# A hybrid decoder step on one core: two plain pairs of gates per layer, branch inputs and adaLN computed under the gate pairs, sigmoids reloaded by GpSimd's queue

## The chip, the cores and the metric

The kernel runs on one core of a Trainium2 chip. The metric is the device time of one execution in microseconds. The core has a matrix engine (TensorE, PE in the profile; PEld is its loading of weights), three engines for element-wise work (VectorE or DVE, ScalarE or ACT, GpSimd or POOL) and SyncE (SP), which only issues transfers here. Each engine runs its own instructions in its own order and waits on semaphores for the others.

## The reference

One inference step of two layers over 1088 tokens (1024 of a prompt, 8 sequences of 8 new tokens), width 1024, all in float32:

```
def _trunk_layer(x, c, ...):
    shift, scale, gate = jnp.split(jax.nn.silu(c) @ w_ada + b_ada, 3, axis=-1)     # adaLN
    h = _rmsnorm(x, norm_g) * (1.0 + scale[:, None]) + shift[:, None]
    (qa, ka, va, ga, ub, vb, gb, qc, fc, ic, gc, ma, mb, mc) = _split_cols(h @ w_in, IN_SIZES)
    ya, ... = _window_attention(...)     # branch A, width 512
    yb = _spatial_gating(ub, vb, w_spatial, b_spatial)     # branch B, width 512
    yc, s_new = _hgrn2(...)     # branch C, width 512
    merged = (jax.nn.sigmoid(ma) * ((ya * jax.nn.silu(ga)) @ w_br_a)
              + jax.nn.sigmoid(mb) * ((yb * jax.nn.silu(gb)) @ w_br_b)
              + jax.nn.sigmoid(mc) * ((yc * jax.nn.silu(gc)) @ w_br_c))
    x = x + gate[:, None] * (merged @ w_out)
```

The parts that the change touches are the merge gates ma, mb, mc (3 x 1024 columns of h @ w_in, then a sigmoid), the gated branch inputs y * silu(g) of the first two branches, adaLN, and the merge.

## The kernel before

**Layout and arithmetic.** Activations lie with channels on the 128 partitions and tokens along the row. The 1088 tokens are cut into three column chunks of 384, 384 and 320 (`CH`). Every float32 product is made of three matmuls in a reduced format (`mm3`, L377 to L379): operands are split into a rounded part and a rest, by a cast on ScalarE and a subtraction on VectorE (`split`, L454 and L455; for weights `piece`, L341 and L342; for branch inputs L1422 and L1423).

**Stages of a layer.** After the branches come three stages. In the *gate stage* 24 tiles of 128 columns are computed in 12 pairs; each result goes through a sigmoid and is stored to DRAM (`put_gate`, L1299 and L1300). Pair e = 0 is plain: 96 matmuls of 384 columns and 48 of 320. Pairs e = 2 to 22 (`gate_pair`) treat the first two column chunks and the two halves of the depth as 2 x 2 blocks and use a Strassen-Winograd scheme with seven block products instead of eight: 84 matmuls of 384 columns and 48 of 320. It needs sums of operand blocks (`sums`, made once per layer on VectorE and POOL and split, tiles `sb`) and, for every pair, sums of its weight blocks (`gate_prefetch`, four operations on POOL, L1340 to L1343, split by `split_t` into tiles `tw`). Tiles `su` hold the partial results; the names u2, u3 and p5 in the code are parts of them.

In the *merge stage* each of the three branches has 8 tiles of 3 column chunks with 12 matmuls each. Its input comes from `load_y`: y and its gate branch g are loaded from DRAM (tiles `yr` and `gr`), multiplied (L1417), and split into tiles `y` or into a spare `H`. The inputs of the first branch are loaded when the gate stage is over, those of the next one under the matmuls of the present one. For each group of 12 matmuls `load_gate` (L1465) reloads a stored sigmoid two groups ahead, VectorE multiplies it with the result (L1496 in the first branch, L1498 later), POOL adds it to `mg` (L1499), and in the last branch the sum is split for the w_out product. In layer 0 the adaLN products of L289 (its own last third and all of layer 1's) run between the merge's matmuls, with weights loaded at L299, and are transposed at L276 after a copy at L272. The *w_out stage* follows.

**What sets the order.** POOL and SP run in the order in which the program is written; a scheduler orders PE, VectorE and ScalarE. All loads and nearly all stores of these stages are issued by SP, so a transfer that waits for data holds back those behind it. Work on the side is a list of generators, `side`; `pump()` advances the first two of them by one step, and `drain()` runs them to their end. Large tiles share 17 slabs (`slab`); raw weights have 4 buffers (`wr`), sigmoids 4 (`gq`), and PSUM has four banks for products and four for other uses.

## Time and profile before

| | us |
|---|---|
| three runs | 2409.55, 2403.61, 2394.68 |
| median | 2403.61 |
| the profiled execution | 2400.19 |
| its span | 2398.4 |
| PE busy | 2277.0 (95%) |
| VectorE, ScalarE, POOL busy | 1293.5, 806.3, 573.7 (54%, 34%, 24%) |
| Strassen pairs of layer 0 and 1 | about 674 to 923, 1877 to 2127 |
| merge of layer 0 and 1 | about 935 to 1145, 2138 to 2298 |

The profile is that of one execution; 1.8 us of its time lie outside the span. Times in its rows are counted from the start of the span. The mean clock granted to PE is 0.983 of full speed. PE's busy time counts a matmul from its start to a modelled end, and matmuls overlap, so the distance between starts tells what one costs, not its duration. A row of stages gives for one stretch of time the busy time of each engine with the number of instructions, then the granted clock, the share of the 16 DMA engines that was busy, and the rate of transfer.

### The profile page before, as it was taken

What the parts mean: (1) busy time and instruction counts of PE and PEld (TensorE: products, weight loads), DVE (VectorE), ACT (ScalarE), POOL (GpSimd) and SP (SyncE); (2) the same over time, 40 slices, a digit from 0 to 9 for tenths busy, and PEclk for the clock granted to TensorE, in tenths of its full rate; (3) what the DMA queues carried; (4) which work ended last, traced back from release to release, by engine and by line L of the source; (5) the groups of instructions that cost most, each with busy time, mean ns of one, the idle gap of its engine ahead of it and who ended that gap; (6) DMA issues with size and microseconds to landing.
All of it is one profiled execution on the core that took longest, in us unless ns stands there. A gap on an engine that the chain in (4) does not pass through costs nothing.

```text
span 2398.4 us, 43921 instructions
## 1 busy us (share of the span) xinstructions
PE 2277.0 (95%) x17402; PEld 2154.5 (90%) x17402; DVE 1293.5 (54%) x2897; ACT 806.3 (34%) x2044; POOL 573.7 (24%) x571
## 2 busy tenths in 40 slices
PE   6999999999989997998999999999999899979999
PEld 5999899989989997777999998999899899979999
DVE  6558656655364444445573586576553644346441
ACT  4445523333134332212233456223331333332220
POOL 3101013242232331133111010132422333212421
PEclk9999999999989998999999999999999899999999
DMA  7222111122123226766432221112221222355451
GB/s 278 75 81 75 62 40 55 57 70 80 58 71 109 93 93 232 238 191 187 163 98 71 82 73 53 51 47 65 63 77 47 89 95 93 106 222 176 132 199 46
DMA packets 140734, 251.31 MB, mean 105 GB/s; under 512 B 19760, under 2 KB 78384, under 8 KB 140496
## 3 DMA queue, kind: packets, MB, share of 16 engines
q1 hardware_dynamic: 129296, 209.96, 27.0%
q0 software_dynamic: 11232, 38.55, 4.5%
q8 instruction: 137, 2.24, 0.4%
q14 instruction: 69, 0.57, 0.1%
HBM read 185.13 MB, written 65.27 MB: 104 GB/s over the span
## 4 chain that ended last, share of the span: by engine, by line
PE 72%; DVE 11%; issue 6%; DMA 5%; POOL 3%; ACT 2%; SPq 1%; POOLq 0%; DVEq 0%; ACTq 0%
PE mm L377 14%; PE mm L378 14%; PE mm L379 14%; PE mm L431 4%; PE mm L433 4%; PE mm L432 4%; PE c L377 3%; PE c L379 3%; PE c L378 3%; DMA wr<-in_w_ada 1%; PE av L912 1%; PE sc L875 1%; POOL mg L1499 1%; DVE pc L342 1%; DMA gr<-y 1%
## 5 line engine op out<-in xcount | busy, mean ns | idle before, releaser
L377 PE MATMUL mm<-H,pc 128*128 128x384 f32 (+1 forms) x1792 | 599.5, 335 | 0.0
L378 PE MATMUL mm<-H,pc 128*128 128x384 f32 (+1 forms) x1792 | 589.4, 329 | 0.0
L379 PE MATMUL mm<-H,pc 128*128 128x384 f32 (+1 forms) x1792 | 588.2, 328 | 0.0
L342 DVE TENSOR_TENSOR pc<-wr,pc 128x512 fp32r<-128x512 f32 x308 | 220.9, 732 | 392.4 <-ACT pc L341 390.9
L377 PEld LDWEIGHTS mm<-H,pc 128*128 128x128 f32 x1792 | 336.7, 188 | 18.1 <-issue 15.1
L378 PEld LDWEIGHTS mm<-H,pc 128*128 128x128 f32 x1792 | 337.0, 188 | 5.6 <-issue 5.0
L379 PEld LDWEIGHTS mm<-H,pc 128*128 128x128 f32 x1792 | 336.6, 188 | 0.9 <-issue 0.4
L341 ACT CAST pc<-wr 128x512 fp32r<-128x512 f32 x312 | 190.2, 620 | 238.0 <-DMA wr<-in_w_br 80.6
L431 PE MATMUL mm<-pc,H 128*128 128x256 f32 x896 | 260.3, 291 | 0.2 <-DVE gq L1148 0.2
L433 PE MATMUL mm<-pc,H 128*128 128x256 f32 x896 | 255.7, 285 | 0.0
L432 PE MATMUL mm<-pc,H 128*128 128x256 f32 x896 | 255.0, 285 | 0.0
L433 PEld LDWEIGHTS mm<-pc,H 128*128 128x128 f32 x896 | 173.1, 193 | 3.2 <-issue 3.2
L431 PEld LDWEIGHTS mm<-pc,H 128*128 128x128 f32 x896 | 173.1, 193 | 2.2 <-DVE gq L1148 0.5
L432 PEld LDWEIGHTS mm<-pc,H 128*128 128x128 f32 x896 | 173.1, 193 | 0.0
L377 PE MATMUL mm<-y,pc 128*128 128x384 f32 (+1 forms) x384 | 132.0, 345 | 39.0 <-ACT y L1422 24.6
L1499 POOL TENSOR_TENSOR mg<-mg,gq 128x384 f32<-128x384 f32 (+1 forms) x96 | 98.9, 1037 | 228.6 <-DVE gq L1498 217.0
L455 DVE TENSOR_TENSOR tw<-wr,tw 128x512 fp32r<-128x512 f32 x88 | 82.7, 975 | 97.0 <-ACT tw L454 97.0
L378 PE MATMUL mm<-y,pc 128*128 128x384 f32 (+1 forms) x384 | 131.3, 342 | 0.3 <-DVE pc L342 0.3
L379 PE MATMUL mm<-y,pc 128*128 128x384 f32 (+1 forms) x384 | 129.2, 336 | 0.0
L377 PEld LDWEIGHTS mm<-y,pc 128*128 128x128 f32 x384 | 74.9, 195 | 46.1 <-ACT y L1422 26.5
L377 PE MATMUL c<-H,pc 128*128 128x320 f32 x352 | 109.6, 311 | 0.0
L379 PE MATMUL c<-H,pc 128*128 128x320 f32 x352 | 109.4, 311 | 0.0
(412 smaller groups left out, 4483.5 us busy)
## 6 DMA issues: line engine op xcount, KB each, us to landing
wr<-in_w_in SPq DMA_DIRECT2D x192, 256.0 KB, 3.6
g<-gq SPq DMA_DIRECT2D x96, 192.0 KB, 1.9
gq<-g SPq DMA_DIRECT2D x96, 192.0 KB, 3.1
wr<-in_w_ada SPq DMA_DIRECT2D x64, 256.0 KB, 3.9
wr<-in_w_in SPq DMA_DIRECT2D x112, 128.0 KB, 2.8
yr<-y SPq DMA_DIRECT2D x24, 544.0 KB, 7.0
wr<-in_w_br SPq DMA_DIRECT2D x48, 256.0 KB, 3.5
gr<-y SPq DMA_DIRECT2D x16, 544.0 KB, 7.9
```

Of the source, the lines that this page charges most:

```text
L341: S.copy(pc[:, 0, :], flat)
L342: eng.tensor_sub(pc[:, 1, :], flat, pc[:, 0, :].bitcast(F32))
L377: T.matmul(ps, w[0], r[0], start=start, stop=False, skip_group_check=True)
L378: T.matmul(ps, w[1], r[0], start=False, stop=False, skip_group_check=True)
L379: T.matmul(ps, w[0], r[1], start=False, stop=stop, skip_group_check=True)
L431: T.matmul(p3(ps), a, wh[k], start=k == 0, stop=False)
L432: T.matmul(p3(ps), a, wl[k], start=False, stop=False)
L433: T.matmul(p3(ps), b, wh[k], start=False, stop=k == 7)
L455: V.tensor_sub(dst_l, src, dst_h.bitcast(F32))
L875: T.matmul(ps[:, j * 256:j * 256 + w], lq, KS[a][hl][:, k0:k0 + w], start=hl == 0, stop=hl == 1)
L912: T.matmul(po[64 * a:64 * a + 64, :], v[:, vt:vt + 64], PT[a][:, c:c + 512], start=hb == 0, stop=hb == nh - 1, tile_position=(0, 64 * a))
L1499: G.tensor_add(mg, mg, sg)
```

## The change

1. Two pairs per layer are plain, e = 0 and e = 2; Strassen pairs are e = 4 to 22. `sums` is advanced once per group of matmuls over both.
2. `gating` computes 0.5 * y * g for the first two branches in 24 chunks per layer and stores the results to new DRAM tiles `yg`; `ada_wide` does adaLN with two column tiles in one matmul (256 columns, half as many instructions), its weights loaded in slabs (`wada`). Both are put on `side` when the Strassen pairs begin, and `pump()` now stands in every product of a pair, nine times per pair. In the merge no adaLN is left, and `load_y` only loads and splits.
3. `first_y` loads and splits the inputs of the first branch inside the last pair, behind the product that is last to use the operand sums.
4. `load_gate` issues the reloads of sigmoids from GpSimd's queue instead of SP's.
5. The last adds of the third branch (j = 7) go to VectorE.

```diff
--- before.py
+++ after.py
@@ -1288,6 +1288,7 @@
 
 
 
+        yg = [dp.tile([4, 128, NTOK], F32, tag=f"yg{l}{b}", name=f"yg{l}{b}") for b in range(2)] + [yd[2]]
         gd = [dp.tile([8, 128, NTOK], F32, tag=f"g{l}{b}", name=f"g{l}{b}") for b in range(3)]
         sbl = []
         HB = H[1]
@@ -1356,13 +1357,15 @@
 
         def gate_pair(e, w, last):
             blk = sbl[0]
+            sb = lambda x: [(blk[k, x, 0], blk[k, x, 1]) for k in range(4)]
+            s2, s3, s4 = [lambda k, x=sb(x): x[k] for x in range(3)]
             a = lambda c, k: (H[c][:, 0, k, :], H[c][:, 1, k, :])
-            sb = lambda x: lambda k: (blk[k, x, 0], blk[k, x, 1])
             full = lambda ps: ps[:, 0:384]
 
             def product(ps, ws, rs, start=True, stop=True):
                 for k in range(4):
                     mm3(ps, ws(k), rs(k), start and k == 0, stop and k == 3)
+                pump()
 
             tmp = slab("su")
             u2, u3, p5 = [tmp[:, x * 384:x * 384 + 384] for x in range(3)]
@@ -1373,14 +1376,17 @@
                 gate_prefetch()
             S.copy(u2, p1)
             x = full(mbank())
-            product(x, t2, sb(0))
+            product(x, t2, s2)
             V.tensor_add(u2, u2, x)
             c21 = full(mbank())
-            product(c21, t3, sb(1))
+            product(c21, t3, s3)
             V.tensor_add(u3, u2, c21)
             x12 = full(bank("c12"))
-            product(x12, lambda k: col(w, 8, 1, k + 4), sb(2))
-            pump()
+            product(x12, lambda k: col(w, 8, 1, k + 4), s4)
+            if last:
+                del blk, s2, s3, s4
+                sbl[:] = []
+                next(ly)
             x = full(mbank())
             product(x, t1, lambda k: a(1, k))
             S.copy(p5, x)
@@ -1406,52 +1412,107 @@
                     product(p1, lambda k: col(w, 8, 0, k + 4), lambda k: a(0, k + 4), start=False)
                     put_gate(e, 0, p1)
 
-        def load_y(b, dst, eng):
-
+        def gating():
+
+            for b in range(2):
+                for kk in range(4):
+                    for c, (t0, n) in enumerate(CH):
+                        t = slab("gy")
+                        y, g = t[:, 0:n], t[:, 384:384 + n]
+                        nc.sync.dma_start(y, yd[b][kk][:, t0:t0 + n])
+                        nc.sync.dma_start(g, yd[3 + b][kk][:, t0:t0 + n])
+                        yield
+                        V.scalar_tensor_tensor(y, y, 0.5, g, ALU.mult, ALU.mult)
+                        nc.sync.dma_start(yg[b][kk][:, t0:t0 + n], y)
+                        del t, y, g
+                        yield
+
+        def ada_wide(l, kts):
+
+            for p in range(0, len(kts), 2):
+                t = [slab("wada")[:, 0:1024].rearrange("p (a c n) -> p a c n", a=2, c=4) for _ in range(2)]
+                for e in range(2):
+                    for a in range(2):
+                        nc.sync.dma_start(t[e][:, a], i["w_ada"][l, kts[p + a]][:, 4 * e:4 * e + 4])
+                yield
+                yield
+                ps = bank("ada")
+                for e in range(2):
+                    for c in range(4):
+                        T.matmul(v3(ps[32 * c:32 * c + 32, 0:256], 128), cT[:, 4 * e + c, :], t[e][:, :, c],
+                                 start=e == 0, stop=e == 1, tile_position=(0, 32 * c))
+                del t
+                yield from ada_rows(l, kts[p:p + 2], ps)
+
+        def load_y(b, dst, first=False):
+
+            def half(y, kk, c):
+                t0, n = CH[c]
+                hi, lo = dst(kk, c)
+                x = y[:, t0:t0 + n]
+                S.copy(hi, x)
+                V.tensor_sub(lo, x, hi.bitcast(F32))
+
+            def load(kk):
+                y = slab("yr")
+                nc.sync.dma_start(y[:, 0:NTOK], yg[b][kk])
+                return y
+            if first:
+                ys = [load(kk) for kk in range(4)]
+                for c in range(3):
+                    for kk in range(4):
+                        half(ys[kk], kk, c)
+                return
             for kk in range(4):
-                y = slab("yr")
-                nc.sync.dma_start(y[:, 0:NTOK], yd[b][kk])
-                if b < 2:
-                    g = slab("gr")
-                    nc.sync.dma_start(g[:, 0:NTOK], yd[3 + b][kk])
-                    eng.tensor_mul(y[:, 0:NTOK], y[:, 0:NTOK], g[:, 0:NTOK])
-                h_ = 0.5 if b < 2 else 1.0
-                for c, (t0, n) in enumerate(CH):
-                    hi, lo = dst(kk, c)
-                    x = y[:, t0:t0 + n]
-                    S.mul(hi, x, h_)
-                    V.scalar_tensor_tensor(lo, x, h_, hi.bitcast(F32), ALU.mult, ALU.subtract)
+                y = load(kk)
+                yield
+                for c in range(3):
+                    half(y, kk, c)
                 yield
 
         def y_slabs():
             t = [[slab("y", F32R) for _ in range(2)] for _ in range(4)]
             return lambda k, c: [x[:, CH[c][0]:CH[c][0] + CH[c][1]] for x in t[k]]
 
+        def first_y():
+            y0.append(y_slabs())
+            for _ in load_y(0, y0[0], True):
+                pass
+            yield
+
+        y0 = []
+        ly = first_y()
+        sg_ = sums()
+        side.append(sg_)
         for e in range(0, 24, 2):
             w = unit()
-            if e == 0:
-                sg_ = sums()
-                side.append(sg_)
-                for j in range(2):
-                    for c in (2, 0, 1):
-                        def ev_s(c, t0, n, ps):
-                            put_gate(j, c, ps)
-                        f_group(w, j, 8, rhs_h, c, ev_s, 2)
-                        if j == 0 and c == 2:
-                            gate_prefetch()
+            if e > 2:
+                gate_pair(e, w, e == 22)
+                continue
+            first_group = True
+            for j in range(2):
+                for c in (2, 0, 1):
+                    def ev_s(c, t0, n, ps):
+                        put_gate(e + j, c, ps)
+                    f_group(w, j, 8, rhs_h, c, ev_s)
+                    if first_group:
+                        (gate_prefetch if e else prefetch)()
+                        first_group = False
+            if e == 2:
                 drain(sg_)
                 for k in range(4):
                     split(HB[:, 0, k, :], HB[:, 1, k, :], sbl[1][k])
                 sbl[1] = None
                 split_t()
-            else:
-                gate_pair(e, w, e == 22)
-        sbl[:] = []
+                side.append(gating())
+                if l == 0:
+                    side.append(ada_wide(0, list(range(16, 24))))
+                if l + 1 < L:
+                    side.append(ada_wide(l + 1, list(range(24))))
         tw[:] = []
+        drain(*side)
         prefetch()
-        rhs_y = y_slabs()
-        ly = load_y(0, rhs_y, V)
-        drain(ly)
+        rhs_y = y0[0]
 
 
         merged, sgs = [], []
@@ -1462,23 +1523,19 @@
                 b, j, c = grp.pop(0)
                 t0, n = CH[c]
                 sgs.append(small("gq", 384, bufs=4)[:, 0:n])
-                nc.sync.dma_start(sgs[-1], gd[b][j][:, t0:t0 + n])
+                nc.gpsimd.dma_start(sgs[-1], gd[b][j][:, t0:t0 + n])
         for _ in range(2):
             load_gate()
         for b in range(3):
             if b == 0:
                 Hy = new_H()
                 rhs_n = lambda k, c, Hy=Hy: (Hy[c][:, 0, k, :], Hy[c][:, 1, k, :])
-                ly = load_y(1, rhs_n, G)
+                ly = load_y(1, rhs_n)
                 side.append(ly)
-                if l == 0:
-                    side.append(ada(0, list(range(16, 24)), True))
             elif b == 1:
                 rhs_n = y_slabs()
-                ly = load_y(2, rhs_n, V)
-                side.insert(0, ly)
-                if l + 1 < L:
-                    side.append(ada(l + 1, list(range(24)), True))
+                ly = load_y(2, rhs_n)
+                side.append(ly)
             else:
                 del Hy
                 Hm = new_H()
@@ -1496,14 +1553,14 @@
                         V.tensor_mul(mg, sg, ps)
                         return
                     V.tensor_mul(sg, sg, ps)
-                    G.tensor_add(mg, mg, sg)
+                    (V if b == 2 and j == 7 else G).tensor_add(mg, mg, sg)
                     if b == 2:
                         split(Hm[c][:, 0, j, :], Hm[c][:, 1, j, :], mg)
                 f_mtile(w, j % 2, 4, lambda c, k: rhs_y(k, c), ev_m)
             if b < 2:
                 drain(ly)
                 rhs_y = rhs_n
-        del rhs_y, rhs_n, merged, ly
+        del rhs_y, rhs_n, merged, ly, y0
         drain(*side)
         last = l + 1 == L
         if not last:
```

The order that results shows at three places. First SP's queue in layer 0, around the loads of weights for pair e = 8 (`wr`); `g` rows are stores of sigmoids. Before:

```order
L1300 DMA g_7362<-gq_8018 128x384
L1300 DMA g_7362<-gq_8046 128x320
L338 DMA wr_8063<-in_w_in 128x512
L338 DMA wr_8068<-in_w_in 128x512
L338 DMA wr_8073<-in_w_in 128x512
L338 DMA wr_8078<-in_w_in 128x512
```

And now, where `gy` are the chunks of y and g, `yg` the product's store and `wada` the adaLN weights:

```order
L1301 DMA g_7364<-gq_8078 128x384
L1301 DMA g_7364<-gq_8106 128x320
L1422 DMA gy_8109<-y_271 128x384
L1423 DMA gy_8109<-y_274 128x384
L1426 DMA yg_7362<-gy_8109 128x384
L1436 DMA wada_8145<-in_w_ada 128x512 x2
L1436 DMA wada_8146<-in_w_ada 128x512 x2
L338 DMA wr_8151<-in_w_in 128x512
L338 DMA wr_8156<-in_w_in 128x512
L338 DMA wr_8161<-in_w_in 128x512
L338 DMA wr_8166<-in_w_in 128x512
```

Two loads, a store that waits for VectorE and four adaLN loads now stand between the stores of a pair and the next weights.

Second, SP's queue at the end of layer 0's gate stage, last Strassen pair to first branch. Before:

```order
L1300 DMA g_7364<-gq_9800 128x384
L1300 DMA g_7364<-gq_9828 128x320
L338 DMA wr_9831<-in_w_br 128x512
L338 DMA wr_9836<-in_w_br 128x512
L1413 DMA yr_9849<-y_271 128x1088
L1416 DMA gr_9851<-y_274 128x1088
```

And now:

```order
L1301 DMA g_7366<-gq_10146 128x320
L1458 DMA yr_10213<-yg_7362 128x1088
L1458 DMA yr_10215<-yg_7362 128x1088
L1458 DMA yr_10217<-yg_7362 128x1088
L1458 DMA yr_10219<-yg_7362 128x1088
L1301 DMA g_7366<-gq_10260 128x384
L1301 DMA g_7366<-gq_10265 128x384
L1301 DMA g_7366<-gq_10281 128x384
L1301 DMA g_7366<-gq_10309 128x320
L1301 DMA g_7366<-gq_10324 128x384
L1301 DMA g_7366<-gq_10352 128x320
L338 DMA wr_10355<-in_w_br 128x512
```

The four loads of the branch input moved ahead of the last pair's six stores; the first branch weight is still behind the last of them.

Third, ScalarE in one Strassen pair of layer 0 (`su` rows are copies of the first and the fifth product; `pc` and `tw` are casts of the next pair's weights and of their sums). Before:

```order
L1374 COPY su_8655<-mm_8656 128x384
L341 CAST pc_8671<-wr_8669 128x512
L341 CAST pc_8676<-wr_8674 128x512
L341 CAST pc_8681<-wr_8679 128x512
L341 CAST pc_8686<-wr_8684 128x512
L454 CAST tw_8774<-wr_8669 128x512
L454 CAST tw_8777<-wr_8684 128x512
L454 CAST tw_8780<-wr_8679 128x512
L1386 COPY su_8655<-mm_8735 128x384
L454 CAST tw_8783<-wr_8674 128x512
L1299 ACTIVATE gq_8750<-su_8655 128x384
```

And now, with the copies of adaLN (`gs`):

```order
L1377 COPY su_8405<-mm_8406 128x384
L272 COPY gs_8431<-ada_8422 128x256
L1392 COPY su_8405<-mm_8529 128x384
L341 CAST pc_8435<-wr_8433 128x512
L341 CAST pc_8440<-wr_8438 128x512
L341 CAST pc_8445<-wr_8443 128x512
L341 CAST pc_8450<-wr_8448 128x512
L1300 ACTIVATE gq_8559<-su_8405 128x384
L272 COPY gs_8527<-ada_8518 128x256
L1300 ACTIVATE gq_8564<-su_8405 128x384
L1300 ACTIVATE gq_8582<-su_8405 128x384
L454 CAST tw_8585<-wr_8433 128x512
```

The weight casts moved from in front of the copy of the fifth product to behind it, and the casts of the sums behind the sigmoid of u3 (`gq_8559`).

## Rows read from the trace of the kernel before

**Rows 1.** Stages: window, us, PE, PEld, DVE, ACT, POOL busy, PEclk, DMA share, GB/s.
```profile
674.00:701.00 27.00, 17.95 (x85) 15.97 (x84) 20.63 (x36) 11.59 (x24) 10.12 (x8) 0.75 0.18 54
701.00:923.00 222.00, 222.00 (x1358) 222.00 (x1357) 86.35 (x129) 81.83 (x161) 62.33 (x49) 1.00 0.30 98
923.00:936.00 13.00, 1.03 (x5) 0.68 (x4) 3.33 (x5) 2.94 (x6) 0.00 (x0) 0.62 0.82 287
...
936.00:1145.00 209.00, 187.60 (x1405) 157.21 (x1405) 110.35 (x227) 48.05 (x101) 59.10 (x51) 0.97 0.68 222
...
1877.00:1905.00 28.00, 18.56 (x87) 16.75 (x86) 20.82 (x36) 11.78 (x24) 9.61 (x8) 0.76 0.17 52
...
2127.00:2138.00 11.00, 0.54 (x4) 0.27 (x2) 2.65 (x3) 2.12 (x5) 0.00 (x0) 0.69 0.78 268
2138.00:2298.00 160.00, 148.97 (x863) 145.45 (x864) 92.76 (x153) 40.58 (x82) 55.30 (x49) 0.97 0.56 182
```

**Rows 2.** Waits of PE, 674 to 702 us: total us, times, longest us.
```profile
PE c L377 <- ACT sb L454: 8.0, 2, 4.9
```

**Rows 3.** Timeline of all engines: start us, us, engine, line, operation [idle before].
```profile
923.03 0.31 PE L379 MATMUL c<-H,pc 128*128 128x320 f32 x1
923.43 0.44 ACT L1299 ACTIVATE gq<-c 128x320 f32<-128x320 f32 x1 [3.02 <-PE c L379]
924.31 0.87 SPq L338 DMA_DIRECT2D wr<-in_w_br  x2
...
927.02 1.25 ACT L341 CAST pc<-wr 128x512 fp32r<-128x512 f32 x2 [3.16 <-DMA wr<-in_w_br]
...
927.67 1.32 DVE L342 TENSOR_TENSOR pc<-wr,pc 128x512 fp32r<-128x512 f32 x2 [12.22 <-ACT pc L341]
...
933.41 1.29 DVE L1417 TENSOR_TENSOR yr<-yr,gr 128x1088 f32<-128x1088 f32 x1 [4.42 <-DMA gr<-y]
...
935.31 0.69 PE L377 MATMUL mm<-y,pc 128*128 128x384 f32 x1 [11.97 <-ACT y L1422]
```

**Rows 4.** Waits of PE, merge of layer 0, 936 to 1145 us.
```profile
PE ada L289 <- DMA wr<-in_w_ada: 14.7, 16, 2.5
```

**Rows 5.** Waits of PE, merge of layer 1, 2138 to 2298 us.
```profile
PE mm L377 <- ACT y L1422: 12.0, 3, 10.6
PE mm L377 <- DVE gq L1498: 4.8, 4, 2.4
```

**Rows 6.** Timeline of PE in the merge of layer 0, adaLN matmuls.
```profile
955.48 0.86 PE L289 MATMUL ada<-wr,cT 128*32 128x128 f32 x24
```

**Rows 7.** Stretches behind a wait of PE in layer 1's merge.
```profile
2158.00:2160.60 2.60, 0.01 (x1) 0.01 (x1) 2.60 (x3) 1.14 (x3) 2.00 (x2) 0.59 0.48 184
2160.60:2165.30 4.70, 4.70 (x15) 4.70 (x16) 4.70 (x7) 1.98 (x6) 2.24 (x1) 0.50 0.63 188
```

**Rows 8.** Timeline of DVE, last branch of layer 1.
```profile
2283.06 0.55 DVE L1498 TENSOR_TENSOR gq<-gq,mm 128x384 f32<-128x384 f32 x1
...
2285.83 0.55 DVE L1498 TENSOR_TENSOR gq<-gq,mm 128x384 f32<-128x384 f32 x1
```

**Rows 9.** DMA issues of the page: operation, count, KB each, us to landing.
```profile
wr<-in_w_in SPq DMA_DIRECT2D x192, 256.0 KB, 3.6
g<-gq SPq DMA_DIRECT2D x96, 192.0 KB, 1.9
...
wr<-in_w_ada SPq DMA_DIRECT2D x64, 256.0 KB, 3.9
yr<-y SPq DMA_DIRECT2D x24, 544.0 KB, 7.0
```

**Rows 10.** Lines of POOL, whole span: busy us, mean ns, idle before.
```profile
L1499 POOL TENSOR_TENSOR mg<-mg,gq 128x384 f32<-128x384 f32 (+1 forms) x96 | 98.9, 1037 | 228.6 <-DVE gq L1498 217.0 <-DVE adaT L279 11.7
```

**Rows 11.** One line: DMAs that POOL issues in the w_out stage.
```profile
L1552 POOL DMA_DIRECT2D x<-x x24: 540/540/600, 1150.6 to 1246.0; - x24
...
DMA to landing us min/median/max: 2.1/2.2/5.2
```


## The prediction

> **What bounds the kernel now.** I read the table of stages first. TensorE (PE) is the engine to look at: in the Strassen part of the gate stage it is busy for all 222 us of 222 at a granted clock of 1.00 (1358 matmuls), while VectorE (DVE) has 86 and GpSimd (POOL) 62 us of work [rows 1]. There only fewer matmuls help. The time that can go lies in three other stretches of each layer: the start of the gate stage, its end, and the merge [rows 1].
>
> One matmul step follows from the first of these: 222.0 / 1358 = 163.5 ns, for a mix of 84 of 384 and 48 of 320 columns per pair (mean 360.7). In proportion to columns that is 174 ns for 384 and 145 ns for 320. A Strassen pair so takes 84 x 0.174 + 48 x 0.145 = 21.6 us, a plain pair 96 x 0.174 + 48 x 0.145 = 23.7 us, and the merge of a layer at full clock 576 x 0.174 + 288 x 0.145 = 142 us.
>
> Start: 674 to 701 us holds 85 matmuls, worth 13.9 us, in 27 us, 13.1 lost; 1877 to 1905 us holds 87, worth 14.2, in 28, 13.8 lost [rows 1]. The waits say why: PE stands 8.0 us in two waits for splits of the operand sums, 4.9 the longest [rows 2]; layer 1 answers with the same row. The rest is clock: 0.75 and 0.76 in the mean over these stretches [rows 1].
>
> End: the timeline shows the last gate matmul start at 923.03, its sigmoid at 923.43, only then SP's branch weight loads at 924.31 and behind them the loads of y and its gate; VectorE multiplies at 933.41, and the first merge matmul starts at 935.31 after 11.97 us idle [rows 3]. In layer 1 the same wait is 10.6 us [rows 5].
>
> Merge: layer 0 takes 209 us for work of 142, layer 1 160 us [rows 1]. Of layer 0's 67 us of excess 14.7 are waits for adaLN weights [rows 4], and about 20 are adaLN's own matmuls: 24 in 0.86 us is 36 ns each [rows 6], 512 of them 18.4, and some 1.6 for the transposes between (an estimate). Layer 1 has no adaLN; its waits are 12.0 for y and 4.8 for the product of the last branch [rows 5].
>
> **The change.** The sum is made against the profiled 2400.2 us (3.4 below the median of 2403.6; the three runs lie within 0.4% of that).
>
> 1. Second plain pair. It removes both starting stalls, since 20.6 us of VectorE, 10.1 of POOL and 11.6 of ScalarE work in that stretch [rows 1] now have 23.7 us more of matmuls above them: -13.1 and -13.8. If this cover fails by the longest single wait, 4.9 us per layer return. The plain pair costs 12 matmuls more: +2.1 per layer. Net -22.7.
>
> 2. First branch inputs earlier. The four loads now stand ahead of the last pair's six gate stores on SP, and their splits ahead of its last sigmoids on ScalarE. What is late next is the branch weight: SP's order leaves it behind the last gate store. From the rows: issued 924.31, cast starts 927.02, two casts take 1.25 and the subtraction behind the first takes about 0.66 (1.32 for two) from 927.67 [rows 3], so the first operand is ready at 928.4. The gap becomes 923.33 to 928.4 = 5.1 us: -6.9 in layer 0, -5.5 in layer 1. Bounds: nothing gained (input splits late again) and all but the 2.7 us of weight landing. I take the middle, since nothing else stands there.
>
> 3. adaLN and the gating under the gate pairs. The merge keeps two losses. After a wait of PE the clock stays low: at 2158 to 2160.6 PE idles and for the 4.7 us behind it is granted 0.50, the lower of its two levels (1.2 instead of 2.4 GHz) [rows 7], which costs half of 4.7, 2.3 us, per gap. And in the last branch one group goes VectorE product, POOL add, ScalarE and VectorE split: 2283.06 to 2285.83 is 2.77 us for a group of 12 x 0.174 = 2.09 [rows 8]. Between the 4.8 us of the wait row [rows 5] and 16 x 0.68 = 11 I take 7, because PSUM's banks cover the first groups. So the merge ends at 142 + 9.3 = 151 us, and the adaLN matmuls, 20 us, move to the gate stage of layer 0.
>
> 4. What the gate stage pays. All of it rests on SP's queue and the DMA engines. In layer 0 the loads sit in six pairs, e = 4 to 14: adaLN 64 x 256 = 16,384 KB, gating 24 x 544 = 13,056 KB (y, gate and the store back, each of eight 544 KB tiles), weights 6 x 1,024 KB, gate stores 6 x 1,088 KB [rows 9]: 42,112 KB, or 43.1 MB. These pairs have 6 x 21.6 + 20 = 150 us. No row shows gate pairs with such traffic. At the 222 GB/s of the present merge the bytes need 194 us, 44 too long; at the 287 of the gap [rows 1] 150, nothing. I take 25, which is 246 GB/s and nearer to the merge's row, because this queue mixes loads and dependent stores as that one does. In layer 1 without adaLN 24.8 MB (gating, and weights and stores of 5.3 pairs) stand against 114 us: 0 at 222 GB/s, 22 at the 182 of its own merge [rows 1]; I take 5, since SP no longer waits for the sigmoid reloads. Below nothing is excluded: no work leaves these pairs.
>
> 5. Reloads from POOL's queue and the last adds on VectorE: nothing. POOL has 1.04 us per add [rows 10] and about 0.54 per DMA issue [rows 11], 1.58 of the 1.97 us that a group takes on average (142 / 72). Without that cover see the third rival.
>
> Sum. Layer 0: -13.1 + 2.1 - 6.9, and merge 209 to 151 with 20 + 25 paid back, -13: -30.9. Layer 1: -13.8 + 2.1 - 5.5, and 160 to 151 with 5 paid back, -4: -21.2. Together -52: 2348 for a profiled run, and 3.4 more for the median, **2352 us**.
>
> **The rivals.**
>
> *Hidden transfers* (chance 0.14). The DMA engines carry 287 GB/s in the gap [rows 1]; if pairs run at that rate, the 25 and 5 us vanish: 2322. Against it: SP's order puts stores that wait for a result between the loads.
>
> *Bound by the queue* (0.18). The gate stage keeps to 222 and 182 GB/s (44 and 22 us instead of 25 and 5), and the end gap stays (12.4 back): 2352 + 19 + 17 + 12 = 2400, no change; with the gap gone, 2388. For it: adaLN loads are late in the merge now [rows 4], where the share of DMA is 0.68 [rows 1]. They would only be late elsewhere.
>
> *POOL's queue sets the merge* (0.08). A reload is issued two groups, 4 us, ahead; an add of 1.04 us may stand before it, and landing takes 2.2 us in the median and 5.2 at most for such a queue [rows 11]. If half a microsecond is missing in each of the 96 groups of the second and third branches: +48, 2400, no change. Against it: these issues took 540 to 600 ns beside a busy VectorE [rows 11].
> The Trainium skill ("SBUF — State Buffer", section "SBUF: two separate sides") speaks against this part of the change: descriptors of a DMA from GpSimd's queue are written by that engine, which a two-port VectorE operation locks out. By its 3100 instead of 620 ns each reload would come 2.5 us later, and an estimate from that would put the merge near this rival or above it; the same page ("Who interferes with whom") takes tensor-tensor operations out of the trap, and by the 600 ns maximum the trace so far agrees with that.
>
> *Slower: stalls that halve the clock in the loaded pairs* (0.09). The place is the preparation of the next pair's weights. SP's order puts their loads behind gating and adaLN loads, and ScalarE's order in layer 0's loaded pairs then puts the four casts behind the copy of the fifth product, and the casts of the weight sums behind a sigmoid that waits for POOL, which has the four sums to make first. PE would meet two late operands per pair, as at 674, and the low clock behind them: 13.1 us [rows 1, 2]. In the 11 pairs that carry loads (six and five) that is 144 us in place of the 30 of step 4: 2352 + 114 = 2466. It is slower by over 1% where these pairs lose 105 / 11 = 9.6 us each. Against it: no pair from 701 to 923 us waits today, with VectorE busy 39% [rows 1], and weight loads have a whole pair of 21.6 us to land.
>
> **How the numbers follow.** My forecast with step 4 between 10 and 50 us in all, 2332 to 2372, has 0.51. One per cent, about what can be told from no change, is below 2379.6 or above 2427.6. Faster: the forecast, the hidden transfers, and a third of the queue's case, 0.70. Slower: nearly all of the last rival, 0.08. The same: 0.22, the rest of the queue's case, POOL's and what lies between. The range from 2316 to 2404 leaves out the best of the hidden case and the slower rival.
>
> **What would show it.** In the new profile: no PE wait at the start of Strassen pairs and a clock of 1.00 there (step 1); 5 us between the last gate and the first merge matmul, ended by the branch weight, not by y (step 2); a merge of about 151 us in both layers with no adaLN line (step 3); waits for adaLN weights or branch loads in layer 0's gate pairs, with DMA near 250 GB/s (step 4); SP's waits for POOL's adds gone and reload landings near 2.2 us (step 5). I am wrong if gate pairs in layer 1 also stretch beyond 22 us, or if the merge keeps over 160 us.

## The result: slower by 1.4%, and the profile after

The changed kernel takes 2436.65 us (median of four runs, 2434.01 to 2438.40) against 2402.70 us before: a ratio of 1.0142, 95% interval 1.0109 to 1.0175. I had forecast 2352 us with a range up to 2404. It came out slower, on the side that I had given 8%.

Below, in the columns of [rows 1], are the stages of the changed kernel's profiled execution (span 2435.4 us): two plain pairs, the Strassen pairs that carry loads, the free ones behind them, the end gap and the merge of layer 0, then the loaded pairs and the merge of layer 1.

```profile
647.00:697.00 50.00, 49.80 (x304) 49.48 (x300) 30.31 (x48) 16.47 (x35) 18.31 (x17) 1.00 0.35 121
697.00:923.50 226.50, 178.69 (x1081) 148.65 (x1082) 72.73 (x181) 56.09 (x119) 37.61 (x30) 0.90 0.58 193
923.50:1007.00 83.50, 83.50 (x511) 83.50 (x511) 33.80 (x56) 32.85 (x67) 21.86 (x18) 1.00 0.36 119
1007.00:1013.40 6.40, 1.09 (x8) 0.82 (x6) 0.00 (x0) 1.05 (x2) 1.07 (x2) 1.00 0.84 256
1013.40:1169.00 155.60, 147.85 (x865) 143.58 (x865) 82.21 (x146) 38.64 (x77) 82.28 (x112) 0.99 0.56 175
...
1921.00:2109.40 188.40, 164.73 (x924) 159.31 (x925) 74.49 (x122) 59.12 (x119) 45.97 (x35) 0.95 0.47 155
...
2177.50:2333.00 155.50, 147.97 (x866) 143.88 (x867) 81.39 (x147) 39.57 (x78) 82.78 (x112) 0.99 0.56 178
```

The start is clean (clock 1.00), the gap is 5 to 6 us (the row of 6.4 us begins before the last gate matmul has ended), both merges last about 155 us. All of that is near the forecast. The loss stands in the second row and in the sixth: six pairs of layer 0 take 226.5 us where six free ones take 129.8, and seven of layer 1 take 188.4 instead of 151.4. The last of these seven carries no gating any more; it starts on operands whose weights were issued at 2068.20, 16 us into the pair before it. Behind these pairs the next ones are full again.

To compare kernels I use one measure from here on: the time from the first product with operand sums of pair e = 4 to that of pair e = 22, nine pairs. The first product with operand sums is also the mark from which I count a pair's start. Before the change nine such pairs without a stall take 194.70 us:

```profile
708.90:903.60 194.70, 194.70 (x1189) 194.70 (x1189) 79.14 (x117) 73.93 (x145) 57.81 (x45) 1.00 0.31 103
```

and in the changed kernel, layer 0 and layer 1:

```profile
697.10:988.40 291.30, 243.56 (x1477) 213.51 (x1478) 98.28 (x220) 80.61 (x166) 57.04 (x45) 0.92 0.52 173
1921.20:2152.70 231.50, 208.03 (x1189) 202.61 (x1190) 91.89 (x148) 75.30 (x150) 58.79 (x45) 0.96 0.44 145
```

The excess is 96.6 us in layer 0, of which about 20 by the forecast's estimate (25 measured, below) are adaLN's own 288 instructions, and 36.8 us in layer 1 with the same 1189 matmuls as before. About 1.6 us of each belong to the two plain pairs and not to the moved work: with the first part of the change alone (run e4, below) these nine pairs take 196.3 us in both layers.

What PE waits for there, first in layer 0 (686 to 924 us), then in layer 1 (1921 to 2153 us):

```profile
PE ada L1442 <- DMA wada<-in_w_ada: 29.8, 12, 8.6
PE ada L276 <- ACT gs L272: 11.1, 5, 3.5
PE mm L378 <- DVE tw L455: 3.5, 2, 1.9
...
PE mm L377 <- DVE su L1383: 11.2, 4, 4.2
PE mm L377 <- ACT tw L454: 7.6, 4, 3.1
```

All rows of these two views together are 47.9 us in layer 0 and 24.0 us in layer 1. In layer 0 nearly all of it is adaLN's own (its weights and the copies of its results); in layer 1 PE waits for the pair's own operands.

And what SP's queue waits for in layer 0 and in layer 1; L1426 is the store of a gated chunk, L1425 its multiplication:

```profile
SPq L1426 <- DVE gy L1425: 69.1, 15, 7.6
SPq L1426 <- DVE adaT L279: 21.8, 3, 9.4
...
SPq L1426 <- DVE gy L1425: 72.7, 21, 7.0
```

One stall of layer 0 shows the chain, in a timeline of all engines (start, length, engine, line, operation, and what ended the idle time before it):

```profile
744.70 1.85 SPq L338 DMA_DIRECT2D wr<-in_w_in  x4
...
753.64 1.42 POOL L1341 TENSOR_TENSOR wr<-wr,wr 128x512 f32<-128x512 f32 x1 [31.61 <-DVE pc L342]
...
759.13 1.00 POOL L1393 TENSOR_TENSOR su<-su 128x384 f32<-128x384 f32 x1
760.16 0.56 DVE L1395 TENSOR_TENSOR su<-su 128x384 f32<-128x384 f32 x1 [5.07 <-POOL su L1393]
...
761.69 0.55 DVE L1425 SCALAR_TENSOR_TENSOR gy<-gy 128x384 f32<-128x384 f32 x1
762.27 0.32 SPq L1426 DMA_DIRECT2D yg<-gy  x1
762.68 1.83 SPq L1436 DMA_DIRECT2D wada<-in_w_ada  x4
...
768.11 1.08 PE L1442 MATMUL ada<-wada,cT 128*32 128x256 f32 x8 [8.58 <-DMA wada<-in_w_ada]
```

Read it backwards. PE idles 8.58 us for adaLN weights. They were issued at 762.68, since SP stood at the store of a chunk. That store waited for a multiplication, which stood in VectorE's order behind the pair's additions; these waited for POOL's addition of u3, and that stood behind POOL's four weight sums. Before these POOL was idle for 31.61 us, to the splits of weights that SyncE had issued only at 744.70, 13.2 us into the pair that began at 731.5. So late weights make the store late, and the late store makes the next loads late.

Behind this wait the granted clock is 0.50, that is 1.2 instead of 2.4 GHz, for 2.8 us:

```profile
768.10:770.90 2.80, 2.79 (x15) 1.99 (x16) 0.00 (x0) 0.00 (x0) 0.00 (x0) 0.50 0.87 317
```

### The profile page after: what moved, and what is told of

It is laid out like the page before. It is cut to its first block, busy times and chain, and to the rows that moved or that the text cites. A ratio compares the mean times of both kernels' runs of the same rounds, so it can differ in the third digit from the quotient of the medians.

```text
span 2435.4 us, 43692 instructions
## 1 busy us (share of the span) xinstructions
PE 2289.6 (94%) x17170; PEld 2159.6 (89%) x17170; DVE 1270.8 (52%) x2925; ACT 794.6 (33%) x2032; POOL 614.2 (25%) x691
## 5 line engine op out<-in xcount | busy, mean ns | idle before, releaser
L377 PE MATMUL mm<-H,pc 128*128 128x384 f32 (+1 forms) x1872 | 624.9, 334 | 3.4 <-ACT pc L341 2.7
L378 PE MATMUL mm<-H,pc 128*128 128x384 f32 (+1 forms) x1872 | 614.8, 328 | 0.6 <-DVE pc L342 0.6
L379 PE MATMUL mm<-H,pc 128*128 128x384 f32 (+1 forms) x1872 | 614.6, 328 | 0.0
L377 PEld LDWEIGHTS mm<-H,pc 128*128 128x128 f32 x1872 | 352.2, 188 | 20.8 <-issue 12.9
L378 PEld LDWEIGHTS mm<-H,pc 128*128 128x128 f32 x1872 | 352.5, 188 | 4.8 <-issue 3.2
L379 PEld LDWEIGHTS mm<-H,pc 128*128 128x128 f32 x1872 | 352.0, 188 | 1.1 <-DVE H L455 0.6
L377 PE MATMUL mm<-y,pc 128*128 128x384 f32 (+1 forms) x384 | 129.3, 338 | 23.9 <-DVE gq L1555 13.4
L1341 POOL TENSOR_TENSOR wr<-wr,wr 128x512 f32<-128x512 f32 x20 | 27.2, 1360 | 409.6 <-DVE pc L342 409.6
L378 PE MATMUL mm<-y,pc 128*128 128x384 f32 (+1 forms) x384 | 126.6, 330 | 0.0
L379 PE MATMUL mm<-y,pc 128*128 128x384 f32 (+1 forms) x384 | 126.4, 329 | 0.0
L629 POOL TENSOR_TENSOR hk<-hk,ht 128x512 f32<-128x512 f32 (+1 forms) x48 | 72.9, 1521 | 129.5 <-issue 38.2
L377 PE MATMUL c<-H,pc 128*128 128x320 f32 x320 | 105.0, 328 | 0.0
L379 PE MATMUL c<-H,pc 128*128 128x320 f32 x320 | 103.6, 324 | 0.0
```

The source lines that it names most:

```text
L377: T.matmul(ps, w[0], r[0], start=start, stop=False, skip_group_check=True)
L378: T.matmul(ps, w[1], r[0], start=False, stop=False, skip_group_check=True)
L379: T.matmul(ps, w[0], r[1], start=False, stop=stop, skip_group_check=True)
L629: G.tensor_mul(kv[:, :, 0, :], kv[:, :, 0, :], bc_in(tv[:, :, 1], m))
L1341: G.tensor_sub(b22, b22, b12)
```

## The experiments

The excess over 194.7 us (nine pairs), from the windows of each profile. In layer 0 adaLN's own instructions are in it.

| run | what it is | layer 0 | layer 1 | us (one run, or median) |
|---|---|---|---|---|
| changed kernel | | 96.6 | 36.8 | 2436.65 |
| e1 | store reads a ready tile | 57.8 | 18.2 | 2381.6 |
| g2 | and the multiplication too | 55.3 | 18.3 | 2380.8 |
| e2 | no gating, no early inputs | 42.4 | 1.6 | 2380.1 |
| e3 | no adaLN | 34.4 | 37.7 | 2401.5 |
| f1 | more distance | 57.6 | 24.7 | 2390.9 |
| f2 | f1, sigmoids by SyncE | 57.1 | 25.8 | 2377.2 |
| h1 | Strassen weights by GpSimd | 65.9 | 18.4 | 2392.1 |
| h2 | f2 and h1 together | 27.6 | 6.8 | 2337.8 |

The kernel before took 2397.81 us on the chip of the e runs, 2402.49 on that of the f runs, 2398.84 (median) with the g runs and 2395.22 with the h runs.

**e1, the store without its wait.** Three theories stood against each other: SyncE's order, bytes, and adaLN's short lead.

```diff
-                        nc.sync.dma_start(yg[b][kk][:, t0:t0 + n], y)
+                        nc.sync.dma_start(yg[b][kk][:, t0:t0 + n], H[c][:, 0, kk, 0:n].bitcast(F32))
```

> Left out: the store of a gated chunk takes its data from a tile of H that is long ready, so the branch inputs are wrong; all loads, multiplications, stores and bytes stay, and only SyncE's wait for VectorE at that store goes. In the changed kernel the six loaded Strassen pairs of layer 0 take 226 us instead of 130 (97 more), the seven of layer 1 188 instead of 151 (37 more). Theory 1 (SyncE's order: a store that waits for VectorE holds back the weight and adaLN loads behind it): 97 falls to 25 to 40, of which 20 are adaLN's matmuls, and 37 to under 10; time about 2350 to 2365. Theory 2 (bytes: the DMA engines can't carry the gating and adaLN traffic in these pairs): both stay within 10 us, time 2425 to 2445. Theory 3 (lead: adaLN's matmuls stand only two products behind their loads, which land too late whatever stands in the queue): 97 falls to 65 to 80 and 37 to under 10, time 2385 to 2400.

The nine pairs of layer 0 and layer 1 in this run:

```profile
697.10:949.60 252.50, 231.23 (x1477) 208.85 (x1478) 101.31 (x220) 81.28 (x166) 57.78 (x45) 0.96 0.60 200
1882.10:2095.00 212.90, 201.22 (x1188) 199.25 (x1189) 94.04 (x148) 75.29 (x150) 58.97 (x45) 0.98 0.48 158
```

With the same bytes, in 39 and 19 us less: the bytes were not the limit (theory 2 falls). But half of layer 1's excess stayed, which neither of the other two had foreseen: both wanted under 10, and layer 0's 57.8 lies between their ranges. Without the wait the loaded pairs of layer 1 behind the first still get their weights 3.0 to 5.6 us behind the mark, where the kernel before has them 1.0 us ahead of it: on SyncE they stand behind stores of sigmoids, at which it waits for 134 us in these nine pairs, and behind chunks.

**e2, without gating.** `gating` and `first_y` are left out, `load_y` is that of the kernel before.

```diff
-                side.append(gating())
-                next(ly)
-        rhs_y = y0[0]
+        rhs_y = y_slabs()
+        ly = load_y(0, rhs_y, V)
+        drain(ly)
```

> The changed kernel without the gating under the gate pairs and without the early load of the first branch's inputs: y and g are loaded and multiplied at the merge as before the change; adaLN stays under the gate pairs, plain pairs and GpSimd's reloads stay. Theory 1 (SyncE's order): without stores that wait for VectorE, layer 0's excess of 97 us falls to 25 to 40 and layer 1's 37 to 0; the end gap is back (+6 per layer): about 2350 to 2365. Theory 2 (bytes): 29.7 instead of 43.1 MB in layer 0's pairs, excess 20 to 45, layer 1 0: about the same time, so this run does not tell 1 from 2. Theory 3 (lead of the adaLN loads): layer 0 keeps 65 to 80, layer 1 0: 2385 to 2405.

Layer 1's excess is gone (1.6 us are what e4 has too), layer 0's is 42.4, just above theory 1's 25 to 40: adaLN by itself costs a little under half of layer 0's. The time, 2380.1, is above theory 1's, mostly because the merges are longer than I had allowed for (165 and 164 us).

**e3, without adaLN.**

```diff
-                if l == 0:
-                    side.append(ada_wide(0, list(range(16, 24))))
-                if l + 1 < L:
-                    side.append(ada_wide(l + 1, list(range(24))))
```

and `ada(..., True)` is back in the merge.

> The changed kernel with adaLN back in layer 0's merge as before the change; gating stays under the gate pairs. Theory 1 (SyncE's order): layer 0's excess falls from 97 to layer 1's size, 30 to 45; its merge grows from 155 by 35 to 50; together 2410 to 2430. Theory 2 (bytes): with 26.8 MB in layer 0's pairs the excess falls to under 10, time about 2385; it would then have to be under 10 in layer 1 too, which measured 37. Theory 3 (lead): as theory 1 within 10 us for layer 0, since gating's own loads are waited for by VectorE.

Gating alone costs 34.4 and 37.7 us, the same in both layers, as theories 1 and 3 said. Layer 0's merge is 178.5 us, 23 longer and not 35 to 50, so the time was 2401.5. e2's 42 and e3's 34 make 77; together they cost 97, so the two hinder each other.

**e4, the two plain pairs alone.**

```diff
-            if e == 0:
+            if e <= 2:
...
+                if e == 0:
+                    continue
```

with `e + j` for `j` in the sigmoid's target, and one step of `sums` per group.

> The kernel before with the first part of the change alone: two plain pairs per layer, operand sums advanced once per group of matmuls. All theories, and the prediction's step 1: 13.1 and 13.8 us of starting stalls go, 2.1 per layer of matmuls come: 2402.7 - 22.7 = 2380, and the gate stages of both layers show a granted clock of 1.00 at the start of the Strassen pairs. If the stall only moves to the second pair, 2400.

2372.87 against 2397.81 on the same chip, one run each: 24.9 us less. The start of layer 0's gate stage has a clock of 1.00 and is nearly full; what is left is one wait of 1.2 us and one of 0.5 us in the first Strassen pair:

```profile
640.00:700.00 60.00, 59.54 (x382) 58.37 (x381) 34.03 (x54) 18.66 (x40) 19.91 (x19) 1.00 0.30 103
```

**f1 and f2, more distance.** In f1 four steps instead of two stand between adaLN's loads and its matmuls, two instead of one ahead of the multiplication, and one between that and its store; f2 also moves the sigmoids' reloads back to SyncE. A chunk of gating so takes three steps instead of two, and the same loads are spread over eight or nine pairs instead of six: f1 can't tell distance from spreading.

```diff
-                yield
-                yield
+                for _ in range(4):
+                    yield
                 ps = bank("ada")
...
+                        yield
                         V.scalar_tensor_tensor(y, y, 0.5, g, ALU.mult, ALU.mult)
+                        yield
                         nc.sync.dma_start(yg[b][kk][:, t0:t0 + n], y)
...
-                nc.gpsimd.dma_start(sgs[-1], gd[b][j][:, t0:t0 + n])
+                nc.sync.dma_start(sgs[-1], gd[b][j][:, t0:t0 + n])
```

> The changed kernel with more distance between a load and its use: adaLN's matmuls four steps behind their loads instead of two, the gating's multiplication two steps behind its loads and its store one step behind the multiplication instead of at once; nothing is left out. After the first runs the theory is: SyncE's order (a store that waits for VectorE ahead of the weights) makes about half of the excess of the loaded pairs, and uses that stand too close behind their loads (TensorE for adaLN weights, VectorE for gating chunks, both in order) make the rest. Then layer 0's excess, summed over all pairs, falls from 97 to 35 to 55 us and layer 1's from 37 to 5 to 20: time 2350 to 2385. If only the wait at the store mattered: as with the ready store, 58 and 19, about 2380. If it is the number of bytes or of instructions: no change, 2425 to 2440.

> The run with more distance, and the sigmoids reloaded from SyncE's queue again. Theory (GpSimd's issues of 0.55 us lengthen the last branch's chain of VectorE, GpSimd, ScalarE, VectorE from the third tile on): the merges fall from 155.5 to 148 to 152 us each, 6 to 14 us less than the run with GpSimd's queue. Rival (the chain is as long without the issues, and something else of the change starts it earlier): merges stay within 2 us.

f1's 2390.9 us is just past the end of its theory's 2385: the excess fell to 57.6 and 24.7, less than I had hoped for. Distance, or the spreading that comes with it, helps, but something else still holds the pairs. In f2 the merges fell from 155.8 and 154.6 to 150.4 and 152.8 us. In layer 0 that is within what was expected; in layer 1 it is the rival's 2 us.

**f3, plain pairs and adaLN with distance, no gating.** It is e2 with four steps of lead and the sigmoids reloaded by SyncE.

> Two plain pairs and adaLN under the gate pairs with its matmuls four steps behind the loads; no gating under the gate pairs, no early load of the first branch, sigmoids reloaded by SyncE. Theory: adaLN's excess in layer 0's pairs falls from 42 to 22 to 30 us (20 of it its matmuls), its merge from 205 (two plain pairs alone) to 160 to 166; against 2372.9 for the plain pairs alone 10 to 25 us less: 2348 to 2363. Rival (adaLN costs the same wherever it stands): 2370 to 2380.

2356.72, as expected. The excess of layer 0 is 35.4, a little above the 30 I had named; the first loaded pair alone is 14.6 us longer, since both adaLN generators start their loads there at once. For 10 us of it the DMA engines are busy 0.92 of the time, at 307 GB/s:

```profile
700.00:710.00 10.00, 8.32 (x67) 6.30 (x66) 1.57 (x3) 0.51 (x2) 0.00 (x0) 1.00 0.92 307
```

So in such a burst bytes can count, though over the nine pairs they do not set the time. The end gap is back (11.1 us for y).

**f5, the fourth part alone.** The kernel before with one edit.

```diff
-                nc.sync.dma_start(sgs[-1], gd[b][j][:, t0:t0 + n])
+                nc.gpsimd.dma_start(sgs[-1], gd[b][j][:, t0:t0 + n])
```

> The kernel before with the fourth part of the change alone: sigmoids reloaded from GpSimd's queue. The prediction's step 5: no change, 2395 to 2402. Theory now: the last branch loses 4 to 8 us per layer, layer 0's adaLN loads win a few since SyncE no longer waits for reload buffers: 2395 to 2412. The prediction's third rival (half a microsecond missing in each of 96 groups): 2440.

2394.5 against 2402.5, one run each: no difference that this can show. Within it the two merges, in the columns of [rows 1], move in opposite directions:

```profile
935.10:1134.80 199.70, 184.80 (x1405) 162.56 (x1406) 114.20 (x229) 47.40 (x102) 94.28 (x120) 0.95 0.73 238
2124.10:2288.00 163.90, 151.03 (x864) 146.03 (x864) 99.57 (x157) 42.23 (x87) 93.18 (x116) 0.97 0.59 192
```

Layer 0's is 10 us shorter than the 209.7 before (PE's waits for adaLN weights in it fall from 14.7 to 6.6 us), layer 1's 3.9 longer than its 160.0.

**g1 and g3, the version that the first runs point to.** g1 is f3 with the third part of the change: y and g of the first branch loaded, multiplied and split inside the last pair. g3 runs adaLN's two generators one after the other.

```diff
                 del blk, s2, s3, s4
                 sbl[:] = []
+                y0.append(y_slabs())
+                drain(load_y(0, y0[0], V))
...
-        rhs_y = y_slabs()
-        ly = load_y(0, rhs_y, V)
-        drain(ly)
+        rhs_y = y0[0]
```

> Two plain pairs, adaLN under the gate pairs with four steps of lead, and now the third part of the change: y and g of the first branch are loaded, multiplied and split inside the last pair, without any gating chunks in other pairs. The prediction's step 2: the end gap falls from about 12 to 5.1 us, ended by the branch weight: 6 to 7 us per layer less than the 2356.7 without it: 2342 to 2348. Rival: VectorE's multiplications wait in its order for their loads ahead of the last pair's additions and stall TensorE there: gap 5, but the last pair longer by as much: 2352 to 2358.

> The run with the early first branch, and adaLN's two generators one after the other instead of side by side: the same 64 loads spread over nine pairs instead of six to seven. Theory (a use too close behind its load, with the low clock behind each wait, makes what adaLN costs above its 20 us of matmuls): layer 0's excess, summed over all pairs, falls from 36 to 22 to 28 us, 8 to 14 us off the time. Rival (it costs the same per step however it is spread): within 4 us.

g1 takes 2330.64 us (four runs) against 2398.84: a ratio of 0.9711, interval 0.9697 to 0.9726. That is better than expected, and better than both kernels. Its pairs of both layers, the last pair of layer 1 and the wait at layer 1's end:

```profile
695.70:923.50 227.80, 220.17 (x1476) 205.10 (x1477) 97.03 (x196) 80.64 (x166) 57.54 (x45) 0.99 0.49 163
1854.30:2050.20 195.90, 195.14 (x1188) 194.82 (x1189) 82.21 (x124) 76.19 (x150) 57.79 (x45) 1.00 0.30 103
2050.20:2071.00 20.80, 19.73 (x122) 19.47 (x120) 11.88 (x19) 8.07 (x19) 1.02 (x1) 1.00 0.73 261
```

```profile
PE mm L377 <- ACT pc L341: 5.1, 1, 5.1
```

The inputs are prepared under one pair without a stall, and the gap ends with the branch weight. g3 (2330.16, ratio 0.9715, interval 0.9699 to 0.9731) gave nothing: its excess is 33.9 against g1's 33.1. Its theory fell: PE's wait for adaLN weights shrank from 5.2 to 3.2 us, but seven of the loaded pairs, now nine, take 24.3 to 25.6 us (the others 28.8 and 27.6): 2.8 us above 21.6, nine times, is 25 us, which is what adaLN's instructions cost without a wait. A pair of h2 (below) shows the same, 24.5 us with PE busy throughout:

```profile
748.40:772.90 24.50, 24.50 (x170) 22.79 (x169) 12.08 (x26) 9.10 (x18) 9.05 (x10) 1.00 0.70 233
```

**g2, ready operands too.** e1, with the multiplication reading H as well, so that VectorE waits for no load of a chunk.

```diff
-                        V.scalar_tensor_tensor(y, y, 0.5, g, ALU.mult, ALU.mult)
+                        x = H[c][:, 0, kk, 0:n].bitcast(F32)
+                        V.scalar_tensor_tensor(t[:, 768:768 + n], x, 0.5, x, ALU.mult, ALU.mult)
```

> The run with the ready store, and the gating's multiplication also reads a ready tile of H: left out is every use of the loaded chunks, so the branch inputs are wrong; loads, multiplications, stores, bytes and adaLN stay. It takes VectorE's wait for the chunk's load away, beside SyncE's wait for VectorE. Theory (that wait, in VectorE's order ahead of the pair's additions, makes the rest of layer 1's excess): 18.6 us of excess in layer 1's pairs fall to under 5, and layer 0's 58 to 38 to 48, adaLN's alone. Rival (the 18.6 are the loads themselves, on the DMA engines or SyncE's queue): both stay within 4 us.

18.3 instead of 18.2 us: the theory fell. In this run VectorE's wait for a chunk was not what held layer 1. The place to look was the weights, by SyncE's timeline: the changed kernel issues the four loads of a pair that began at 1945.5 behind a store at 1954.54,

```profile
1954.54 0.32 SPq L1426 DMA_DIRECT2D yg<-gy  x1
1955.27 1.84 SPq L338 DMA_DIRECT2D wr<-in_w_in  x4
```

g2 those of a pair that began at 1931.7 behind chunks of gating,

```profile
1935.80 0.62 SPq L1423 DMA_DIRECT2D gy<-y  x1
1936.52 1.84 SPq L338 DMA_DIRECT2D wr<-in_w_in  x4
```

and the kernel before those of a pair that begins at 2064.6 a microsecond ahead of it:

```profile
2063.59 2.92 SPq L338 DMA_DIRECT2D wr<-in_w_in  x4
```

The loaded pairs of layer 1 behind the first, in e1 and g2 together, lengthen with this lateness: they take 21.6 and 22.0 us where the loads are issued 1.4 and 3.0 us behind the mark, 23.0 to 23.5 us at 3.8 to 4.1, and 24.3 to 26.5 us at 4.8 to 5.6.

**h1 and h2, the weights out of SyncE's queue.**

```diff
-            nc.sync.dma_start(d, src)
+            (nc.sync if keep is None else nc.gpsimd).dma_start(d, src)
```

`keep` is given for the Strassen pairs' weights alone. h1 is the changed kernel with this edit, h2 is f2 with it.

> The changed kernel with one edit: the Strassen pairs' weights are loaded from GpSimd's queue, so they no longer stand behind gating loads, gating stores and gate stores on SyncE; nothing is left out. Theory 4 (what holds the pairs is that SyncE issues the weights late: then come casts, four sums on GpSimd, the addition of u3 behind them, and its sigmoid, whose store holds SyncE again): layer 1's excess falls from 37 to under 10 us, layer 0's from 97 to 45 to 70, where adaLN's late loads stay: time 2360 to 2400. Rival (VectorE's gating operations, in its order ahead of the pair's additions, hold the pairs): layer 1 stays at 18 or more, time above 2400.

> The run with more distance and SyncE's reloads, and the Strassen pairs' weights loaded from GpSimd's queue. Theory 4: layer 1's excess over all pairs falls from 27 to under 8, layer 0's from 56 to 25 to 40: 2330 to 2350, near the version that leaves the gating out (2330.6). Rival (VectorE's order): layer 1 stays at 18 or more, time 2360 to 2380.

The nine pairs of both layers, of h1:

```profile
699.60:960.20 260.60, 234.61 (x1478) 207.59 (x1477) 93.82 (x215) 78.61 (x161) 72.92 (x77) 0.95 0.57 189
1896.80:2109.90 213.10, 200.16 (x1189) 197.49 (x1189) 89.22 (x144) 73.28 (x148) 73.76 (x77) 0.98 0.48 153
```

and of h2:

```profile
697.90:920.20 222.30, 218.43 (x1477) 203.87 (x1477) 98.70 (x210) 78.67 (x161) 74.86 (x77) 1.00 0.69 222
1853.60:2055.10 201.50, 196.96 (x1191) 196.32 (x1190) 92.63 (x144) 74.79 (x148) 75.26 (x77) 0.99 0.50 162
```

h1 leaves 18.4 us in layer 1, by its own expectation the rival's number, while layer 0's 65.9 and the time of 2392.1 are theory 4's. Its weights come in time (issued at 1940.57 for a pair that begins at 1945.2). What PE waits for in layer 1 is VectorE; VectorE waits for chunks, and SyncE can load a chunk only behind the store of the one before, where it waits for VectorE:

```profile
PE mm L377 <- DVE su L1383: 12.7, 6, 4.0
...
DVE gy L1425 <- DMA gy<-y: 55.0, 22, 4.4
...
SPq L1426 <- DVE gy L1425: 63.0, 23, 5.9
```

h2, with the weights moved and the distance, leaves 6.8 (theory 4's number) and 27.6, and takes 2337.8 us. Its weights for a pair that begins at 1899.4 are issued 11.6 us ahead of it:

```profile
1887.78 2.15 POOL L338 DMA_DIRECT2D wr<-in_w_in  x4
```

So neither edit is enough alone: with the weights on SyncE they come late (e1, g2, f1), and with the store right behind its multiplication the chunks come late (h1). With both edits the same gating and adaLN bytes run at 222 GB/s in layer 0 at a granted clock of 1.00, and the 27.6 us are nearly the 25 of adaLN's own instructions.

## Why the prediction was wrong

**Step 4 failed**, what the gate stage pays for the moved work. It took 25 us in layer 0 and 5 in layer 1, worked out from bytes and transfer rates. Measured are 96.6 - 20 = 77 and 36.8: 52 and 32 us more than forecast (5 of the 52 are adaLN's own instructions, 25 us where I had estimated 20). Bytes were the wrong yardstick, as e1 and h2 show: the same bytes fit into 252 and 222 us instead of 291. What costs is the order on one in-order queue: stores that wait for VectorE, ahead of adaLN's weights (layer 0), of the pairs' weights and of the next chunks. The clock adds to the stalls: its mean over the loaded stretches was 0.90 and 0.95. An estimate from these rows for layer 0: 47.9 us of waits and 25 of adaLN's own instructions leave 24 of the 96.6, and a mean of 0.90 over 226.5 us is 45 us at the lower level, which cost up to half of that.

This is the place that my slower rival named (weights behind gating and adaLN loads on SyncE, sums and u3 on POOL), with 0.09 of the chance. Its price, 13.1 us for each loaded pair, is near what layer 0 paid, 77 / 6 = 12.8, but that is partly luck: the rival had PE wait for two late operands of the pair, and 40.9 of layer 0's 47.9 us of waits are for adaLN's weights and copies. Layer 1, where PE does wait for the pair's operands, paid 36.8 / 7 = 5.3, and six of its pairs carried chunks, not five. I weighed the rival low because no Strassen pair waits in the profile before; but before, nothing that waits for a result of the pair stood ahead of the weights except the gate stores, and the weights were issued a microsecond ahead of the pair. That slack was the number to read: the order of SyncE showed two loads, a store and four loads put into it. My other argument, that weight loads have a whole pair of 21.6 us to land, was wrong. POOL makes the sums of the new weights in front of the present pair's addition of u3, and in the profile before, in the pair that begins at 882.0, that addition starts 0.76 us behind the last sum. What it waits for is the copy of the fifth product, which stands in ScalarE's order behind casts of these sums:

```profile
892.79 1.67 ACT L454 CAST tw<-wr 128x512 fp32r<-128x512 f32 x3 [5.33 <-POOL wr L1342]
...
894.91 1.26 POOL L1387 TENSOR_TENSOR su<-su 128x384 f32<-128x384 f32 x1 [0.76 <-ACT su L1386]
```

So weights that come later make u3 later in the same pair, and VectorE's additions behind it. PE did not stall at once: the pairs of e1 and g2 above had room for 2 to 4 us.

**Step 1 was right.** e4 alone gave 24.9 us, forecast 22.7, and layer 0's start shows a clock of 1.00 and 0.46 us without PE at work in 60.

**Step 2 was right.** PE waits at the end, for the branch weight, in layer 0 5.37 us (5.1 forecast) and in layer 1 5.2:

```profile
1008.17 0.44 ACT L1300 ACTIVATE gq<-c 128x320 f32<-128x320 f32 x1 [3.02 <-PE c L379]
1009.01 1.87 SPq L338 DMA_DIRECT2D wr<-in_w_br  x4
...
1013.46 1.01 PE L377 MATMUL mm<-y,pc 128*128 128x384 f32 x2 [5.37 <-ACT pc L341]
```

**Step 3 was nearly right.** The merges take about 155 us instead of 151. In the last branch of layer 0 every group, the narrow ones too, takes the chain's time, as POOL's rows show: 1140.51 to 1143.14 to 1145.97.

```profile
1140.51 1.00 POOL L1556 TENSOR_TENSOR mg<-mg,gq 128x384 f32<-128x384 f32 x1 [1.19 <-DVE gq L1555]
...
1143.14 1.25 POOL L1556 TENSOR_TENSOR mg<-mg,gq 128x320 f32<-128x320 f32 x1 [1.12 <-DVE gq L1555]
```

**Step 5 was right in f5's sum, not in its parts.** f5 shows no change in the total, made of two opposite ones. The reloads on GpSimd's queue were not free: f5's merge of layer 1 is 3.9 us longer by them, and f2, which takes them off again, has merges of 150.4 and 152.8 us, close to the 151 of step 3. So most of what step 3 missed came with step 5. The third rival's 48 us did not happen. The issues on GpSimd's queue stayed short, and the landings took 2.7 us in the median and 7.0 at most, where SyncE's took 2.7 and 10.1 before:

```profile
L1526 POOL DMA_DIRECT2D gq<-g x144: 537/554/580, 1005.8 to 2333.8; - x144
...
DMA to landing us min/median/max: 2.4/2.7/7.0
```

The Trainium skill's trap ("SBUF — State Buffer", "SBUF: two separate sides"), by an estimate from that section's 3100 and 620 ns, would have made issues or landings some 2.5 us longer. Beside the tensor-tensor operations of this merge neither the longest issue, 580 ns, nor the median landing shows it, which agrees with the same page's section "Who interferes with whom" in the Trainium skill, where a probe with tensor-tensor operations did not stall a DMA.

Together: 2352 + 52 + 32 + 8 for the two merges = 2444, against 2436.65. Of the difference of 7 us 2 are step 1's; the rest, about 5 us, is not traced and near the 4.4 us by which the four runs differ.

Left open: how much of h2's gain comes from the distance alone once the weights are off SyncE, since no run with the weights moved has ready operands; and how much of it is the spreading over more pairs that the distance brings (g3, which spreads adaLN's loads alone, gained nothing; no run spreads the gating alone). The runs of e, f and h and g2 are one execution each, so differences of a few us between their times show nothing. A version with h2's weights and g1's early inputs was not run either.

## What to carry to other kernels

Before moving loads and stores under a full stage, ask of each in-order queue which instruction waits for a result of that stage, and what that the stage needs stands behind it; then read how early the stage's own loads are issued today and how long what they feed stands ready before it is needed. Counting bytes against a rate comes second. Put loads that a pair cannot start without on a queue that carries no dependent stores, and keep a step or more between an operation and the store of its result; h2 did both, at 6.8 instead of 36.8 us in layer 1.

## What was not expected

Two holds on the same pairs did not add. Layer 1 lost 36.8 us. Either of two edits alone (e1, h1) left 18, and a third (g2 beside e1) left that unchanged; distance alone (f1) left 24.7, and distance with the weights moved (h2) left 6.8. A remainder that an experiment leaves unchanged is no proof that the thing it removed costs nothing: it may cost only when the other is gone.

The last pair hid more than the forecast had asked of it: in g1 the first branch's eight loads of 544 KB, their multiplications and splits run under it at 261 GB/s, with PE busy for 19.73 of 20.8 us.
